# A macaron decoder layer in split fp32: the spatial output is computed earlier and parked in DRAM, and eight pairs of the mixer's merge run on seven products at three units a block

## The chip, the cores and the metric

The kernel runs on one core of a Trainium2 chip. The metric is the device time of one execution in microseconds. The version before takes 1982.98 us, the median of three runs (1982.88 to 1983.88). One more execution was profiled.

## The reference

One layer of a hybrid decoder on 256 tokens of width 2048, in float32:

```
x = x + 1/2 * SwiGLU_1(rms(x))              # D_FF = 5632
h = rms(x); h @ w_in -> q | k | v | u | v_sg | gate_att | gate_sg
    A: causal dilated window attention, 3 groups of 4 heads (dilations 1, 4, 16),
       partial rotary, the groups of a head slot merged by their softmax denominators
    B: u * (W_s LN(v_sg) + b), W_s lower-triangular, 12 groups      @ w_sg_out -> y_sg
x = x + (sigmoid(gate_att) * (A @ w_att_out) + sigmoid(gate_sg) * y_sg) @ w_out
x = x + 1/2 * SwiGLU_2(rms(x)); final RMSNorm
```

Nearly all of the work is in the matrix products. x stays in SBUF for the whole layer; the weights are read from DRAM once, in order.

## The kernel before, in words

**A product.** TensorE (PE) multiplies in a reduced fp32 format. To keep fp32 accuracy each weight tile w is split on the chip into wh, a rounded copy made by ScalarE (ACT, L356), and wl = w - wh, made by VectorE (DVE, a subtraction recorded at the helper line L66). The activations are split into xhi and xlo in the same way. A product is then three matmuls, wh x xhi, wl x xhi and wh x xlo, each with 512 output columns in one PSUM bank (`product`, L363). A *unit* is one weight tile of 128x512.

**Gemms and steps.** `gemm` notes each matrix product as a row of column blocks of 512; `lay_out` then writes the whole program as one list of steps. A plain step ("n") covers two units and both token halves: 12 matmuls. One such step is one *tick*; callbacks are hung at ticks with `at(tick, fn)`. The engines run their instructions in the order in which this loop issues them, and so does SP, which issues nearly all the DMAs.

**Quads.** Two gemms on the same activations and a run of k tiles form a 2x2 block product: two token halves, two column blocks, two k halves. `quad_products` runs it in the Strassen-Winograd way on seven products p1 to p7 in place of eight. `nq` says how many pairs of k tiles the blocks hold; the rest of the pair's k tiles run as plain steps in between. A product is one "s" step of nq units and 3 x nq matmuls. The blocks of weights lie in a *home* (room in SBUF); DVE makes four further forms of them (`prepare`: f, t2, t1, t4, recorded as `sum<-quads`, `quads<-sum,quads` and the like), and forms of the activations are made by `sums_of` when x is turned. ACT and DVE also move three of the partial results between PSUM banks and a small tile (`read` in `quad_products`); p5 may only begin when DVE has read p7's bank. Opening products (p1, p6, p7) are put some steps ahead of the pair's own first step, closing ones (p5, p4, p3, p2) into it.

**The ring.** wh and wl live in a ring of nine units (`RING`). `advance` splits steps a few ahead of PE as long as the ring's room is free, that is, as PE has gone past the units that lay there. Raw weights come in by SP two units at a time (512 KB, L256), five such tiles ahead (`RAWB`); quad blocks come in by `load_block` (L298).

**Turns.** x, and other matrices that PE needs transposed, go through DRAM: DVE transposes blocks of 32 (`btx<-x`), SP writes them out (`bmx<-btx`) and reads them back with the blocks exchanged (`xt<-bmx`), ACT scales them, and ACT and DVE split them into xhi and xlo.

**The mixer.** Column blocks of w_in in the order vs, u (with a home of their own, `gates`), q and k of three groups, v, then for each chunk c of 512 columns gs, w_sg_out, ga, w_att_out; then w_out. `merge` is the second home: gs/ga for c = 2, 3 and the two pairs of w_out run there as quads with nq = 2. Attention (`attention`, L938 ff.) starts 16 ticks behind the last k and takes a head slot every five ticks: scores into two banks (`qk`, recorded as sc, L951), `softmax` (DVE and ACT), the turn of p through DRAM, ten ticks later the product with v (`pv`, L986 ff.) into one bank, and a tick behind that the split of the result into oT (`oev`). All these banks come in turn from `tp_bank`, four of the eight PSUM banks.

Of the kernel before, what the change touches and what calls it, by code (L numbers as in the profile page):

```python
# [18 lines left out]
P = 128  # L19
# [20 lines left out]
CS = (2, 0, 0)  # L40
CM = 2
# [30 lines left out]
def layer(ctx: ExitStack, tc: tile.TileContext, a, out):  # L72
# [10 lines left out]

    def tp_bank(name):
        return ps.tile([P, NC], F32, tag="tp", bufs=4, name=name)
# [11 lines left out]

    rows = sb.tile([64, P], F32, name="rows")
# [15 lines left out]
    x = big.tile([P, NT, D], F32, name="x")  # L114
    xv = a["x"][0].rearrange("(t p) d -> p t d", p=P)

    def load_x(c0, c1):
        SP.dma_start(x[:, :, c0:c1], xv[:, :, c0:c1])
# [26 lines left out]
    def opening(count):  # L145
        return zip((5, 3, 1) if count > 9 else (4, 2, 1), ("p1", "p6", "p7"))

    def lay_out():
        i, count = 0, 0
        while i < len(gemms):  # L150
# [23 lines left out]
            count = len(order) if size > 1 else 16  # L174
# [87 lines left out]
    def ffn_home(home):  # L262
        home["h"] = [big.tile([P, 16, S], F32R, tag=tag, name=f"h{tag}") for tag in "AB"]
# [12 lines left out]
    def merge_home(home):  # L276
        l_ = sb.tile([P, 3, 2, NC], F32, tag="L", name="quads")
        w = sb.tile([P, 3, NC], F32, tag="W", name="part")
        t = sb.tile([P, 2, NC], F32, tag="tmp", bufs=2, name="sum")
        return l_[:, 0], l_[:, 1], l_[:, 2], w[:, 1:3], t, l_[:, 0], w[:, 0]  # L280

    def move_in(home):
        home["room"] = home["make"](home)
        for b in (0, 2, 3, 1):
            load_block(next(q for q in quads if q["home"] is home), b)
# [107 lines left out]
    def quad_products(i, quad, form):  # L393
# [5 lines left out]
        for q in range(quad["nq"]):  # L399
# [6 lines left out]
            else:  # L406
                hi, lo = (v[:, ("p5", "p6", "p7", "p3").index(form)] for v in quad["forms"]["forms"][q])
# [111 lines left out]
    def norm_squares(n, c):  # L519
        for t in range(NT):  # L520
            ACT.activation(junk, x[:, t, c * NC:(c + 1) * NC], AF.Square, accum_out=ss[n][:, t, c:c + 1])
# [18 lines left out]
    def first_transposes(k):  # L540
        b = first_place(k)
        for t in range(NT):
            PE.transpose(b[:, t * P:(t + 1) * P], x[:, t, k * P:(k + 1) * P], ident)
# [5 lines left out]

    def residual(e, n, c, banks, scale, norm):  # L550
        cs = slice(c * NC, (c + 1) * NC)

        def add():
            for t in range(NT):
                DVE.scalar_tensor_tensor(two(x[:, t, cs]), banks[t], scale, two(x[:, t, cs]),
# [11 lines left out]

        turn_x(e + (6 if c == 1 else 2), n, c, (9 if n == 1 else 7) if c == 3 else 6)

    def turn_x(i, n, c, lag, read=3):  # L570
        def evac(src):
# [6 lines left out]
            if c == CS[n]:  # L578
                sums_of(i + lag, xT, 0, 2, forms_tile(big, "oT", f"fx{n}", 2), src, f"x{n}", tag)
            elif n != 1 and c == CS[n] + 1:  # L580
                sums_of(i + lag, xT, 2, 1, forms_tile(big, "k2", f"fy{n}", 1), src, f"y{n}", tag)

        turn(i, f"x{n}_{c}", 8, put_tokens(lambda: x[:, :, c * NC:(c + 1) * NC]),
# [8 lines left out]
    def ffn(wg, wu, wd, down_post, group):  # L592
# [7 lines left out]
        def lhs_h():  # L600
            return home["h"]

        for after, (part, quads_of) in zip(GATES, enumerate(PARTS)):
            for f in range(*after):
# [13 lines left out]
                def post_up(e, banks, st=st, f=f, kl=kl, quads_here=quads_here):  # L618
# [11 lines left out]
                    def ev(src):  # L630
                        hi, lo = (v[:, kl:kl + 4] for v in home["h"])
# [19 lines left out]
                quad = dict(k0=4 * CS[n], nq=2 if late else 3, forms=xT, home=merge if late else home)  # L651
                gemm(wg, f * NC, 0, KD, lhs_x, post_gate, BOTH if f else LATE, bank, quad)
                gemm(wu, f * NC, 0, KD, lhs_x, post_up, BOTH, bank, quad)
            for c in range(4):
                if c % 2 == 0:
                    bank = side()
                    quad = dict(k0=quads_of["k0"], nq=quads_of["nq"], forms=sets[part], home=home)
# [143 lines left out]
    def spatial(e):  # L801
        for pg in range(6):
            got = {}

            def prod(pg=pg, got=got):
                if pg == 0:
                    both = [big.tile([P, 16, S], F32R, tag=tag, name=f"uT{tag}") for tag in "BA"]
                    mix["uT"] = [v[:, 0:NG] for v in both]
                    mix["fs"] = [v[:, NG:].rearrange("p f (q t) -> p f q t", q=2) for v in both]
# [29 lines left out]
    def post_qk(key, gi):  # L839
        def post(e, banks):  # L840
# [4 lines left out]
            if (key, gi) == ("q", 0):  # L845
                parts = big.tile([P, 4, one], F32R, tag="E", name="qk0")
                kept = xT["both"]

                def keep():
                    for new, old in zip(mix["fs"], kept):  # L850
                        ACT.activation(new, old.bitcast(F32), AF.Copy)
                    mix["forms"] = {q: [v[:, :, q] for v in mix["fs"]] for q in range(2)}
# [3 lines left out]
            elif (key, gi) == ("q", 1):  # L856
# [3 lines left out]
                mix["q", 2] = sb.tile([P, one], F32, tag="W", name="q2")  # L860
# [77 lines left out]
    def attention(e):  # L938
        for s in range(NSLOT):
            got = {}  # L940
            e0 = e + 5 * s
# [3 lines left out]
            def qk(s=s, got=got):  # L945
                got["b"] = [tp_bank(f"sc{s}_{r}") for r in range(2)]
# [31 lines left out]
            def pv(s=s, got=got):  # L978
                bank = got["o"] = tp_bank(f"pv{s}")
# [18 lines left out]
            for k, f in ((0, qk), (1, softmax), (10, pv), (11, oev)):  # L998
# [3 lines left out]
    def post_sig(key):  # L1002
# [20 lines left out]
    def post_merge(c):  # L1023
        def post(e, banks):
# [11 lines left out]
            def ev(src):  # L1036
                split_psum(turned(mix["mhi"][:, 4 * c:4 * c + 4]), turned(mix["mlo"][:, 4 * c:4 * c + 4]), src, c < 2)
                if c == CM:
                    sums_of(e + 10, mix, 0, 2, lambda: mix["fs"], src, "m", "tmp")
# [6 lines left out]
    for j, (c0, post) in enumerate(front):  # L1046
# [3 lines left out]
        if j % 2 == 0:  # L1050
            bank = side()
            quad = dict(k0=4 * CS[1], nq=2, forms=xT, home=gates)
# [4 lines left out]
    for gi in (1, 2, 0):  # L1057
        gemm(w_in, o_v + gi * NC, 0, KD, lhs_x, post_v(gi))
    sg_out = lambda: mix["uT"]
    att_out = lambda: (mix["oT"][:, 0], mix["oT"][:, 1])  # L1060
    for c in range(4):
        if c < 2:
            bank = (mm_bank, tp_bank)[c]
            gemm(w_in, o_gs + c * NC, 0, KD, lhs_x, post_sig("gs"), bank=bank)
            gemm(a["w_sg_out"][0], c * NC, 0, NG, sg_out, post_mul("gs"), bank=bank)
            gemm(w_in, o_ga + c * NC, 0, KD, lhs_x, post_sig("ga"), bank=bank)
        else:
            sides[0] += c == 2
            bank = side()
            quad = dict(k0=4 * CS[1], nq=2, forms=mix, home=merge)  # L1070
            gemm(w_in, o_gs + c * NC, 0, KD, lhs_x, post_sig("gs"), BOTH, bank, quad)
            gemm(w_in, o_ga + c * NC, 0, KD, lhs_x, post_sig("ga"), BOTH, bank, quad)
            gemm(a["w_sg_out"][0], c * NC, 0, NG, sg_out, post_mul("gs"), bank=bank)
        gemm(a["w_att_out"][0], c * NC, 0, NSLOT, att_out, post_merge(c), bank=bank)
    for c in range(4):
        if c % 2 == 0:
            bank = side()
            quad = dict(k0=4 * CM, nq=2, forms=mix, home=merge)
        gemm(a["w_out"][0], c * NC, 0, KD, lambda: (mix["mhi"], mix["mlo"]),
             lambda e, banks, c=c: residual(e, 2, c, banks, 1.0, True), PAIR if c == 0 else BOTH, bank, quad)  # L1080

# [4 lines left out]
    def down2(e, c, banks, last):  # L1086
# [5 lines left out]
        def add():  # L1092
            if c == 0:
                ss[3] = sb.tile([P, NT, 5], F32, name="ss3")
            for t in range(NT):
                DVE.scalar_tensor_tensor(two(x[:, t, cs]), banks[t], 0.5, two(x[:, t, cs]),
                                         op0=OP.mult, op1=OP.add)
            norm_squares(3, c)
            for t in range(NT):
                DVE.tensor_tensor(x[:, t, cs], x[:, t, cs], fin["g"][:, cs], op=OP.mult)  # L1100
# [9 lines left out]
    def finish(t):  # L1110
# [3 lines left out]
        for q, cs in enumerate((a_, b_)):  # L1114
            DVE.scalar_tensor_tensor(x[:, t, cs], bank[:, q], 0.5, x[:, t, cs], op0=OP.mult, op1=OP.add)
# [196 lines left out]
```

## Time and profile before

| | |
|---|---|
| median of 3 runs | 1982.98 us |
| profiled execution | 1985.29 us |
| span in the profile | 1983.5 us |
| mean granted TensorE clock | 0.999 of full |
| PE / PE weight loads / DVE / ACT / POOL busy | 99 / 87 / 80 / 60 / 3% |
| DRAM traffic | 461 MB read, 30 MB written, 247 GB/s |

The profiled execution takes 1.8 us more than its span. In a view of groups each row gives line, engine, operation, output and inputs by the program's names, how often it occurs, its busy time and the mean ns of one, and then the idle time ahead of these instructions with what ended it. In a timeline each row gives start and length in us; a bracket is the idle time before the row and what released it. Rows of the trace are of the profiled execution.

### The profile page before, as it was taken

To read this page: it belongs to the slowest core of one execution; us is meant where nothing else is said; L and a number is where in the kernel's file an instruction comes from. 1 tells how busy PE (TensorE), PEld (TensorE's weight loads), DVE (VectorE), ACT (ScalarE), POOL (GpSimd) and SP (SyncE) were. 2 spreads that over 40 slices of the span, in tenths; PEclk is the share of its full clock that TensorE was granted. 3 is DMA by queue.
4 is the path that set the end of the run, shared out by engine and by line. 5 is a ranking of instruction groups with operands and counts; after the bars stand their busy time and mean duration, and the time that the engine had idled before them with its cause. 6 is when DMAs were issued, how large, how long until landed. Compare 5 with 4: busy or idle time off the path is not lost.

```text
span 1983.5 us, 25183 instructions
## 1 busy us (share of the span) xinstructions
PE 1971.1 (99%) x9188; PEld 1723.6 (87%) x9188; DVE 1592.2 (80%) x1655; ACT 1189.5 (60%) x1382; POOL 51.7 (3%) x48
## 2 busy tenths in 40 slices
PE   9999999999999999999999999999999999999998
PEld 8888888888888888888888888878888888888887
DVE  6798888888897798766665777888898889888886
ACT  7566556665666676555454555576655566565664
POOL 0000100000000000000000000000000000000000
PEclk9999999999999999999999999999999999999999
DMA  9788778787777985888877667788888777878783
GB/s 323 256 279 271 237 238 266 247 254 245 247 242 226 289 294 186 254 275 255 264 238 249 210 204 231 237 260 267 255 252 260 234 249 247 252 250 254 244 265 123
DMA packets 264644, 492.34 MB, mean 248 GB/s; under 512 B 17484, under 2 KB 46024, under 8 KB 264392
## 3 DMA queue, kind: packets, MB, share of 16 engines
q1 hardware_dynamic: 253624, 469.49, 72.0%
q0 software_dynamic: 10576, 20.71, 6.0%
q8 instruction: 72, 1.18, 0.2%
q10 hardware_dynamic: 320, 0.53, 0.1%
q14 instruction: 52, 0.43, 0.1%
HBM read 461.01 MB, written 29.66 MB: 247 GB/s over the span
## 4 chain that ended last, share of the span: by engine, by line
PE 95%; DVE 2%; DMA 1%; issue 1%; ACT 0%; SPq 0%; POOLq 0%; POOL 0%; DVEq 0%; ACTq 0%
PE qd L363 71%; PE mm L363 22%; DVE wl L66 1%; DMA raw<-in_w_in_dram 0%; DMA quads<-in_w_in_dram 0%; DVE btx L66 0%; ACT wh L356 0%; PE sp L815 0%; PE warm L1180 0%; DMA xt<-bmx 0%; DVE xlo L66 0%; PE pv L990 0%; PE sc L953 0%; DVE x L66 0%; DVE quads L66 0%
## 5 line engine op out<-in xcount | busy, mean ns | idle before, releaser
L66 DVE TENSOR_TENSOR wl<-raw,wh 128x1024 fp32r<-128x1024 f32 (+1 forms) x636 | 695.7, 1112 | 184.5 <-ACT wh L356 182.8
L356 ACT ACTIVATE wh<-raw 128x1024 fp32r<-128x1024 f32 (+1 forms) x636 | 609.1, 966 | 365.8 <-PE qd L363 199.6
L363 PE MATMUL qd<-wh,xlo 128*128 128x512 f32 x1201 | 455.4, 379 | 1.0 <-DVE xlo L66 1.0
L363 PE MATMUL qd<-wh,xhi 128*128 128x512 f32 x1201 | 455.3, 379 | 0.0
L363 PE MATMUL qd<-wl,xhi 128*128 128x512 f32 x1201 | 455.2, 379 | 0.0
L356 ACT ACTIVATE wh<-quads 128x1536 fp32r<-128x1536 f32 (+2 forms) x226 | 250.9, 1117 | 271.1 <-PE qd L363 251.5
L66 DVE TENSOR_TENSOR wl<-quads,wh 128x1536 fp32r<-128x1536 f32 (+2 forms) x226 | 291.0, 1301 | 147.7 <-ACT wh L356 147.5
L363 PEld LDWEIGHTS qd<-wh,xlo 128*128 128x128 f32 x1201 | 227.0, 189 | 33.9 <-DVE xlo L66 1.8
L363 PEld LDWEIGHTS qd<-wh,xhi 128*128 128x128 f32 x1201 | 227.0, 189 | 32.4 <-issue 0.2
L363 PEld LDWEIGHTS qd<-wl,xhi 128*128 128x128 f32 x1201 | 227.0, 189 | 32.2
L363 PE MATMUL mm<-wh,xlo 128*128 128x512 f32 x608 | 230.6, 379 | 0.9 <-DVE xlo L66 0.8
L363 PE MATMUL mm<-wh,xhi 128*128 128x512 f32 x608 | 231.1, 380 | 0.1
L363 PE MATMUL mm<-wl,xhi 128*128 128x512 f32 x608 | 228.5, 379 | 0.0
L363 PE MATMUL qd<-wh,hA 128*128 128x512 f32 x564 | 213.8, 379 | 0.0
L363 PE MATMUL qd<-wl,hA 128*128 128x512 f32 x564 | 213.8, 379 | 0.0
L363 PE MATMUL qd<-wh,hB 128*128 128x512 f32 x564 | 213.8, 379 | 0.0
L356 ACT ACTIVATE wh<-sum 128x1024 fp32r<-128x1024 f32 (+2 forms) x85 | 101.4, 1196 | 86.7 <-PE qd L363 66.9
L66 DVE TENSOR_TENSOR wl<-sum,wh 128x1024 fp32r<-128x1024 f32 (+2 forms) x85 | 117.8, 1395 | 18.0 <-ACT wh L356 16.5
L363 PEld LDWEIGHTS mm<-wh,xlo 128*128 128x128 f32 x608 | 114.9, 189 | 17.8 <-DVE xlo L66 1.6
L363 PEld LDWEIGHTS mm<-wh,xhi 128*128 128x128 f32 x608 | 114.9, 189 | 16.2 <-ACT xhi L547 0.2
L363 PEld LDWEIGHTS mm<-wl,xhi 128*128 128x128 f32 x608 | 114.9, 189 | 16.1
L363 PE MATMUL qd<-wh,fx 128*128 128x512 f32 x352 | 119.2, 379 | 1.0 <-DVE part L66 1.0
(417 smaller groups left out, 2191.2 us busy)
## 6 DMA issues: line engine op xcount, KB each, us to landing
raw<-in_w_in_dram SPq DMA_DIRECT2D x168, 512.0 KB, 4.9
raw<-in_ffn_w_down_dram SPq DMA_DIRECT2D x120, 512.0 KB, 5.0
raw<-in_ffn_w_up_dram SPq DMA_DIRECT2D x112, 512.0 KB, 6.0
raw<-in_ffn_w_gate_dram SPq DMA_DIRECT2D x111, 512.0 KB, 4.2
quads<-in_ffn_w_gate_dram SPq DMA_DIRECT2D x38, 768.0 KB, 6.4
quads<-in_ffn_w_up_dram SPq DMA_DIRECT2D x38, 768.0 KB, 5.1
quads<-in_ffn_w_down_dram SPq DMA_DIRECT2D x32, 512.0 KB, 5.4
quads<-in_ffn_w_up_dram POOLq DMA_DIRECT2D x17, 768.0 KB, 10.6
```

The lines of the kernel that those rows point to most:

```text
L66: return method(out, *args, **kwargs)
L356: ACT.activation(wh, r[:, first:end], AF.Copy)
L363: PE.matmul(g["ps"][t], act, in_turn(w), start=not g["begun"][t], stop=g["left"][t] == 0, skip_group_check=g["quad"] is not None)
```

## The change

**Order.** The four w_sg_out gemms run ahead of the second q. Their results y go to DRAM (`post_sg`, four tiles yd of 512 KB) and come back one chunk at a time (`load_y`), to be multiplied with sigmoid(gs).

**Room.** x is written to DRAM chunk by chunk at the end of FFN1 (`out_x`), its SBUF room holds forms of x during the mixer (`forms_room`, filled in part by copies in `keep`), and x is read back behind the last gs (`load_old_x`, four times 512 KB). The home `merge` moves from three small tiles to the two large ones A and B, which w_sg_out has left; q2 and y lie in the rest of B.

**Quads.** merge now has eight pairs, all with nq = 3: q2/k2, v1/v2, the four gs/ga and the two of w_out. With it go 48 of 9022 matmuls of 512 columns; 48 units more are split on ACT and DVE. In `prepare` and the splits, 70 more DVE instructions have 1536 columns and 47 fewer have 1024. The x forms for the mixer's quads are made from chunks 2 and 3 in place of 0 and 1 (`CS`), those for w_out from 1 and 2 in place of 2 (`CM`).

**Attention.** It starts 13 ticks behind the last k, takes a head every four ticks, and `tp_bank` is split: scores and pv share the two banks of `lo_bank`, the other two are `hi_bank`. Behind pv of heads 2 and 3 stands one matmul of constants into the unused half of the bank.

```diff
-CS = (2, 0, 0)
-CM = 2
+CS = (2, 2, 0)
+CM = 1
...
+    halves = [0]
+
     def tp_bank(name):
-        return ps.tile([P, NC], F32, tag="tp", bufs=4, name=name)
+        halves[0] += 1
+        return (lo_bank, hi_bank)[(halves[0] - 1) // 2 % 2](name)
+
+    def lo_bank(name):
+        return ps.tile([P, NC], F32, tag="tp", bufs=2, name=name)
+
+    def hi_bank(name):
+        return ps.tile([P, NC], F32, tag="tq", bufs=2, name=name)
...
     def opening(count):
+        if count == 4:
+            return zip((2, 1, 0), ("p1", "p6", "p7"))
...
     def merge_home(home):
-        l_ = sb.tile([P, 3, 2, NC], F32, tag="L", name="quads")
-        w = sb.tile([P, 3, NC], F32, tag="W", name="part")
-        t = sb.tile([P, 2, NC], F32, tag="tmp", bufs=2, name="sum")
-        return l_[:, 0], l_[:, 1], l_[:, 2], w[:, 1:3], t, l_[:, 0], w[:, 0]
+        a_, b_ = (big.tile([P, 4096], F32, tag=tag, name=f"quads{tag}") for tag in "AB")
+        t = sb.tile([P, SGW], F32, tag="W", name="sum")
...
+        home["left"] = b_[:, 2 * SGW:]
+        return b11, b21, b12, b22, t2, b11, a_[:, 2 * SGW:2 * SGW + NC]
...
+        if n == 1:
+            def out_x():
+                old_x[c] = m = dram.tile([P, NT, NC], F32, tag=f"xd{c}", name=f"xd{c}")
+                SP.dma_start(m, now_x[0][:, :, cs])
+
+            at(e + 5, out_x)
...
-                attention(e + 16)
-                at(e + 16 + 15 + 12, lambda: move_in(merge))
+                attention(e + 13)
+                at(e + 29, lambda: load_y(0))
...
-            e0 = e + 5 * s
+            e0 = e + 4 * s
...
-                got["b"] = [tp_bank(f"sc{s}_{r}") for r in range(2)]
+                got["b"] = [lo_bank(f"sc{s}_{r}") for r in range(2)]
...
-                bank = got["o"] = tp_bank(f"pv{s}")
+                bank = got["o"] = lo_bank(f"pv{s}")
...
+                if s > 1:
+                    PE.matmul(bank[:, S:NC], ones[:, 0:P], ones[:, 0:S], start=False, stop=True, skip_group_check=True)
...
-            for k, f in ((0, qk), (1, softmax), (10, pv), (11, oev)):
+            o = max(10, 12 - 4 * s)
+            for k, f in ((0, qk), (1, softmax), (o, pv), (o + 1, oev)):
...
+            at(e + 1, go)
+            at(e + 2, lambda: SP.dma_start(m, y))
+            if c == 3:
+                at(e + 1, lambda: move_in(merge))
...
+            if key == "gs":
+                at(e + 2, lambda: DVE.tensor_tensor(t_, t_, mix["y"], op=OP.mult))
+                if c < 3:
+                    at(e + 4, lambda: load_y(c + 1))
+                else:
+                    at(e + 1, lambda: load_old_x(e + 1))
...
-    for gi in range(3):
+    for gi in range(2):
+        if gi == 1:
+            for c in range(4):
+                gemm(a["w_sg_out"][0], c * NC, 0, NG, sg_out, post_sg(c), bank=(lo_bank, hi_bank, mm_bank, mm_bank)[c])
...
+    quad = x_quad()
+    gemm(w_in, o_q + 2 * NC, 0, KD, lhs_x, post_qk("q", 2), BOTH, tp_bank, quad)
+    gemm(w_in, o_k + 2 * NC, 0, KD, lhs_x, post_qk("k", 2), BOTH, tp_bank, quad)
...
+    for gi in (1, 2):
+        gemm(w_in, o_v + gi * NC, 0, KD, lhs_x, post_v(gi), BOTH, mm_bank, quad)
+    gemm(w_in, o_v, 0, KD, lhs_x, post_v(0), bank=hi_bank)
     for c in range(4):
...
+        quad = x_quad()
+        gemm(w_in, o_gs + c * NC, 0, KD, lhs_x, post_sig("gs", c), BOTH, bank, quad)
+        gemm(w_in, o_ga + c * NC, 0, KD, lhs_x, post_sig("ga", c), BOTH, bank, quad)
...
-            quad = dict(k0=4 * CM, nq=2, forms=mix, home=merge)
+            bank = (mm_bank, tp_bank)[c // 2]
+            quad = dict(k0=4 * CM, nq=3, forms=lambda: mix, home=merge)
```

**What moves.** PE where the scores of head 3 are formed (pv is a head's product with v, sc_0 and sc_1 are the two banks of its scores, mm is a plain gemm, qd a quad's bank). Before, between two plain steps, with pv of head 1 ahead of them:

```order
L363 MATMUL mm_1_7307<-wh,xlo_4564 128x512
L986 MATMUL pv_7465<-pTk,vq 128x256
L987 MATMUL pv_7465<-pTk,vq 128x2x64
L990 MATMUL pv_7465<-pTk,vq 128x128 x4
L951 MATMUL sc_0_7472<-qk_6004 128x256 x3
L953 MATMUL sc_0_7472<-pTk,vq 128x128
L953 MATMUL sc_0_7472<-k_6346,q_6345 128x128
L951 MATMUL sc_1_7473<-qk_6004 128x256 x3
```

Now, with pv of head 0 ahead of them and p5 of the first gs/ga quad ahead of that:

```order
L377 MATMUL qd_3_7624<-wh,fy_5175 128x512
L1025 MATMUL pv_7841<-pTk,vq 128x256
L1026 MATMUL pv_7841<-pTk,vq 128x2x64
L1029 MATMUL pv_7841<-pTk,vq 128x128 x4
L990 MATMUL sc_0_7848<-qk_6020 128x256 x3
L992 MATMUL sc_0_7848<-pTk,vq 128x128
L992 MATMUL sc_0_7848<-k_6787,quadsB 128x128
L990 MATMUL sc_1_7849<-qk_6020 128x256 x3
```

The bank of sc_1 is now that of pv_7841, a few rows ahead of it; sc_0 has the other of the two.

DVE where the result of pv of head 0 is read (oT<-pv; p is a head's scores in SBUF, btp their transposed blocks). Before, from the end of head 1's softmax:

```order
L66 TENSOR_SCALAR p_7255<-p_7255,ar_7262 128x512 x2
L66 TENSOR_TENSOR wl<-raw_7168,wh 128x1024
L66 TENSOR_TENSOR wl<-raw_7188,wh 128x1024
L66 STREAM_TRANSPOSE btp_7298<-p_7255 128x8x4x32
L66 TENSOR_TENSOR wl<-raw_7206,wh 128x1024
L66 COPY pTk<-p_7137 128x512
L66 TENSOR_TENSOR wl<-raw_7235,wh 128x1024
L66 TENSOR_TENSOR wl<-raw_7266,wh 128x1024
L66 TENSOR_TENSOR oT<-pv_7340,oT 128x2x128
```

Now, from the end of head 2's softmax:

```order
L66 TENSOR_SCALAR p_7772<-p_7772,ar_7779 128x512 x2
L66 TENSOR_TENSOR wl<-quadsA,wh 128x512
L66 TENSOR_TENSOR wl<-quadsA,wh 128x1024
L66 TENSOR_TENSOR wl<-raw_7634,wh 128x1024
L66 TENSOR_TENSOR quadsA<-quadsA,qd_3_7624 128x512
L66 STREAM_TRANSPOSE btp_7822<-p_7772 128x8x4x32
L66 TENSOR_TENSOR wl<-sum,wh 128x1536
L66 TENSOR_TENSOR wl<-raw_7665,wh 128x1024
L66 TENSOR_TENSOR wl<-raw_7709,wh 128x1024
L66 TENSOR_TENSOR qd_2_7623<-qd_3_7624,quadsA 128x512
L66 TENSOR_TENSOR oT<-pv_7841,oT 128x2x128
```

The same read comes one head later, and steps of a quad (quadsA, sum, qd) stand among the splits.

SP at the start of the mixer, around the last quarter of x (xt_3) and the load of the first quad's blocks. Before:

```order
L256 DMA raw_4969<-in_w_in_dram 128x2x512
L482 DMA xt_3_4989<-bmx_3_4927 32x4x256 x4
L256 DMA raw_4994<-in_w_in_dram 128x2x512
L298 DMA quads<-in_w_in_dram 128x2x512 x4
L256 DMA raw_5017<-in_w_in_dram 128x2x512
```

Now:

```order
L268 DMA raw_4975<-in_w_in_dram 128x2x512
L592 DMA xd_4995<-x 256x1x512
L496 DMA xt_3_4997<-bmx_3_4925 32x4x256 x4
L268 DMA raw_5002<-in_w_in_dram 128x2x512
L312 DMA quads<-in_w_in_dram 128x2x512 x4
L268 DMA raw_5025<-in_w_in_dram 128x2x512
```

The write of x's last quarter (xd) stands ahead of both; that of the third quarter stands ahead of xt_2 in the same way.

More of the change, by code (lines that the diff above doesn't have):

```diff
@@ L846, in post @@
                 parts = big.tile([P, 4, one], F32R, tag="E", name="qk0")
-                kept = xT["both"]
+                kept, room = xT["fx"], xT["forms_room"]
                 def keep():
-                    for new, old in zip(mix["fs"], kept):
-                        ACT.activation(new, old.bitcast(F32), AF.Copy)
-                    mix["forms"] = {q: [v[:, :, q] for v in mix["fs"]] for q in range(2)}
+                    for k in range(2):
+                        ACT.activation(room[:, k, :, 0:2], kept[k].bitcast(F32), AF.Copy)
+                    xT["kept"] = dict(forms={q: [room[:, k, :, q] for k in range(2)] for q in range(3)})
                 at(e + 4, keep)
@@ L1051, in layer, with x_quad @@
             bank = side()
-            quad = dict(k0=4 * CS[1], nq=2, forms=xT, home=gates)
+            quad = dict(k0=4 * CS[1], nq=2, forms=lambda: xT, home=gates)
         gemm(w_in, c0, 0, KD, lhs_x, post, BOTH, bank, quad)
-    for gi in range(3):
+    sg_out = lambda: mix["uT"]
+    att_out = lambda: (mix["oT"][:, 0], mix["oT"][:, 1])
+    def x_quad():
+        return dict(k0=4 * CS[1], nq=3, forms=lambda: xT["kept"], home=merge)
+    for gi in range(2):
+        if gi == 1:
+            for c in range(4):
+                gemm(a["w_sg_out"][0], c * NC, 0, NG, sg_out, post_sg(c), bank=(lo_bank, hi_bank, mm_bank, mm_bank)[c])
@@ L1173, in layer @@
     wb = tp_bank("warm")
-    ones = nc.const_aps.tensor(1.0, [P, NC], BF16)
     def keep_warm(count, w=NC):
```

117 lines of the change are left out of this document (68 added, 49 removed).

## The prediction

> **What bounds the kernel now.** The profile's page was read first: the span, the busy shares of the engines, and the chain that ended last.
>
> ```profile
> span 1983.5 us, 25183 instructions
> PE 1971.1 (99%) x9188; PEld 1723.6 (87%) x9188; DVE 1592.2 (80%) x1655; ACT 1189.5 (60%) x1382; POOL 51.7 (3%) x48
> PE 95%; DVE 2%; DMA 1%; issue 1%; ACT 0%; SPq 0%; POOLq 0%; POOL 0%; DVEq 0%; ACTq 0%
> ```
>
> A busy PE is not yet a PE at its limit, so the next view is the chain of waits in order of time, for the distance between matmuls in a long unbroken piece, and then what PE waited for in the whole run (us in total, times, longest).
>
> ```profile
> 96.55 543.91 PE qd L363 x2520
> ```
> ```profile
> PE qd L363 <- DVE part L66: 1.0, 1, 1.0
> PE qd L363 <- DVE xlo L66: 1.0, 2, 0.8
> ...
> PE mm L363 <- DVE xlo L66: 0.8, 1, 0.8
> PE qd L363 <- DVE wl L66: 0.6, 1, 0.6
> ```
>
> 543.91 us for 2520 matmuls is 0.2158 us each, without a break. The waits on DVE sum to 3.4 us. So PE sets the time: a matmul taken out is worth 0.2158 us, as long as no engine that feeds PE comes late. Whether one does is read by stage. Columns: busy time of PE, PEld, DVE, ACT and POOL, granted clock, DMA share, GB/s.
>
> ```profile
> 660.00:680.00 20.00, 20.00 (x95) 17.50 (x93) 12.23 (x13) 14.55 (x24) 0.00 (x0) 1.00 0.91 279
> 680.00:700.00 20.00, 19.16 (x89) 16.48 (x88) 14.45 (x17) 11.05 (x16) 1.10 (x1) 1.00 1.02 351
> 960.00:980.00 20.00, 20.00 (x101) 17.72 (x100) 14.48 (x20) 11.13 (x18) 0.00 (x0) 1.00 0.78 243
> 1000.00:1020.00 20.00, 20.00 (x108) 17.91 (x107) 13.22 (x16) 11.28 (x16) 0.00 (x0) 1.00 0.74 206
> 1040.00:1100.00 60.00, 60.00 (x280) 52.54 (x279) 37.70 (x38) 28.63 (x32) 0.00 (x0) 1.00 0.72 234
> 1240.00:1290.00 50.00, 50.00 (x233) 43.80 (x232) 42.67 (x47) 30.19 (x38) 0.00 (x0) 1.00 0.76 236
> 1310.00:1330.00 20.00, 18.37 (x83) 15.48 (x84) 19.96 (x27) 17.72 (x29) 0.00 (x0) 1.00 0.79 237
> ```
>
> The clock is full throughout. Attention (960 to 1020) and the gates behind it leave DVE a quarter to a third idle; the end of w_out (1240) leaves 15%; the step into FFN2 (1310) leaves nothing, and there PE already loses 1.6 us. The start of the mixer (680) is bound by DMA: a share of 1.02, and PE loses 0.8 us.
>
> **The change, part by part.** *Matmuls.* A pair on seven products saves 3 x nq matmuls. Four pairs at nq 2 become eight at nq 3: 72 saved in place of 24, so 48 fewer, 48 x 0.2158 = 10.4 us, less 0.2 for the two small constant matmuls: **-10.1 us**. The row above prices a matmul. The Trainium skill, TensorE: Matmul & The Clock Gate, Back-to-back issue gap, gives a sustained 131 ns for a matmul of 512 columns in a stream with weight loads, and 216 only for one by itself. By 131 ns the 48 would be worth an estimated 6.3 us; this trace runs 2520 of them in such a stream at 216, so the measured price stands.
>
> *DVE and ACT.* A pair that becomes a quad of nq 3 costs 9 more units of 512 columns on both engines and four prepares on DVE. The groups by line, with shapes kept apart (busy us, mean ns):
>
> ```profile
> L66 DVE TENSOR_TENSOR wl<-raw,wh 128x1024 fp32r<-128x1024 f32 x506 | 613.5, 1222 | 179.7 <-ACT wh L356 177.9
> L66 DVE TENSOR_TENSOR wl<-quads,wh 128x1536 fp32r<-128x1536 f32 x88 | 154.6, 1757 | 105.0 <-ACT wh L356 105.0
> ...
> L66 DVE TENSOR_TENSOR wl<-raw,wh 128x512 fp32r<-128x512 f32 x130 | 84.5, 685 | 4.9 <-ACT wh L356 4.9
> ...
> L66 DVE TENSOR_TENSOR sum<-quads 128x1536 f32<-128x1536 f32 x23 | 40.3, 1752 | 0.0
> ...
> L66 DVE TENSOR_TENSOR oT<-pv,oT 128x256 fp32r<-128x256 f32 x4 | 1.9, 469 | 3.9 <-ACT oT L461 3.9
> ```
> ```profile
> L356 ACT ACTIVATE wh<-quads 128x1536 fp32r<-128x1536 f32 x88 | 130.5, 1483 | 179.1 <-PE qd L363 177.5 <-PE mm L363 1.7
> ```
>
> Now attention, for one head on DVE and on PE (start, length):
>
> ```profile
> 958.89 1.35 DVE L66 SCALAR_TENSOR_TENSOR p<-sc,mask 128x512 f32<-128x512 f32 x2
> 960.28 1.22 DVE L66 TENSOR_REDUCE am<-p 128x2 f32<-128x1024 f32 x1
> 963.08 0.17 DVE L66 RECIPROCAL ar<-am 128x2 f32<-128x2 f32 x1 [1.59 <-ACT p L964]
> 963.28 0.88 DVE L66 TENSOR_SCALAR p<-p,ar 128x512 f32<-128x512 f32 x2
> 965.17 2.36 DVE L66 TENSOR_TENSOR wl<-raw,wh 128x1024 fp32r<-128x1024 f32 x2 [1.01 <-ACT wh L356]
> 967.45 1.24 DVE L66 STREAM_TRANSPOSE btp<-p 128x1024 f32<-128x1024 f32 x1
> ```
> ```profile
> 957.75 0.52 PE L951 MATMUL sc<-qk 128*128 128x256 f32 x3
> ...
> 958.47 0.60 PE L951 MATMUL sc<-qk 128*128 128x256 f32 x3
> ...
> 959.27 0.46 PE L363 MATMUL mm<-wh,xhi 128*128 128x512 f32 x1
> ```
> ```profile
> 986.86 0.59 PE L986 MATMUL pv<-pTk,vq 128*128 128x256 f32 x2
> ...
> 988.33 0.60 PE L951 MATMUL sc<-qk 128*128 128x256 f32 x3
> ```
>
> Two 1024-column splits take 2.36 us, not 2.44: in a row, each starts 0.08 us before the last one's end. So a step of DVE is 1.14 us at 1024 columns, 1.67 at 1536, 0.60 at 512, 1.16 for the transpose; a softmax holds DVE from 958.89 to 964.16, 5.2 us with its wait for ACT. On PE a head's scores take 1.52 us (half of them 0.72) and pv 1.47.
>
> *Attention is the large term.* In the new order the second half of head 3's scores goes into the bank that pv of head 0 has just filled, so PE must wait until DVE has read it (the oT row). DVE gets there in its own order. The work before it begins with the split of p1 of the first gs/ga quad, whose room in the ring of nine comes free when PE reaches head 0's scores. From there to the oT row, by the new order: seven instructions of 1536 columns (4 splits, 3 prepares) 11.7 us, eight of 1024 9.1, seven of 512 4.2, three softmaxes 15.6, three transposes 3.5, a copy and the oT step 0.8: 44.9, and 1.5 for ACT's copy ahead of the first. PE meanwhile has 144 matmuls 31.1, three heads' scores 4.6, pv 1.5 and half of head 3's scores 0.7: 37.9. PE waits 46.4 - 37.9 = **8.5 us**; its p5 step just ahead of that waits for the same queue, so this is counted once. Before, heads came every five ticks, the steps between were plain ones, and four banks took turns. Low end: without the three waits of 1.59 for ACT, 3.7. High end: a wait for ACT's weight copy of 1.0 behind each softmax, as at 965.17, 11.5. The sum is nearest to the middle. The Trainium skill, Perfetto Trace Analysis, Matmuls, asks for groups to rotate through PSUM banks so that one's evacuation lies beside the next one's matmuls, which speaks against four banks becoming two. The rule by itself would price only the exposed evacuation, some 0.5 us of DVE by the oT row; here the queue ahead of the evacuation is the cost.
>
> *Start of the mixer.* Four transfers of 512 KB write x to DRAM; the last two stand on SP ahead of the last x turns and of the four quad loads, in the stretch where DMA is full.
>
> ```profile
> 671.69 1.71 ACT L574 ACTIVATE xt<-xt,gcols 128x256 f32<-128x256 f32 x4 [3.67 <-DMA raw<-in_w_in_dram]
> ...
> 689.22 1.06 ACT L356 ACTIVATE wh<-quads 128x1024 fp32r<-128x1024 f32 x1 [6.24 <-DMA quads<-in_w_in_dram]
> ```
>
> At 351 GB/s one is 1.5 us, two 3.0. ACT already waits here for both. The sums for the x forms, now from chunks 2 and 3, fall into this stretch too, but DVE idles 5.5 of 20 us there. From 0 to 5 us; I take half of the two transfers, **+1.5**.
>
> *Gates and w_out.* A gs/ga pair with its att_out is 207 matmuls, 44.7 us. At the share of the row at 1040 (0.63) DVE works 28.1 us of that; 9 units (half of 1.14 each, 5.1) and four prepares (4 x 1.67, 6.7) make it 39.9, a share of 0.89, little above the 0.85 that the row at 1240 bears without a stall. y's reading back and its product with the gate (one 1024-column step a chunk) lie in the same gaps; the transfers have a DMA share of 0.72 to hide in. **+0.5**, from 0 to 3. Moving the spatial output ahead, ACT's 16 copies more and the second reading of x are covered likewise (ACT 60% busy, PE never waiting for it between 720 and 1300).
>
> *Step into FFN2.*
>
> ```profile
> 1298.54 1.23 DVE L66 TENSOR_TENSOR wl<-raw,wh 128x1024 fp32r<-128x1024 f32 x1 [4.16 <-ACT wh L356]
> ...
> 1326.75 0.68 DVE L66 TENSOR_TENSOR part<-part,qd 128x512 f32<-128x512 f32 x1
> ```
>
> From 1298.54 on DVE has no idle time up to the last wait of PE. The second w_out quad at nq 3 adds four times 0.53 for the prepares, three units (1.7), and takes 0.6 from PE's time: up to 4.4 us. A part of it lies before 1298, where DVE is idle for 4.16 us: **+1.5**, from 0 to 4.4.
>
> Sum: -10.1 + 8.5 + 1.5 + 0.5 + 1.5 = +1.9 us.
>
> **The rivals.** *The full gain.* Attention's wait does not form, because DVE, a third idle there now, has worked ahead. Against it: the ring holds nine units, so DVE cannot be ahead by more than those, and the sum starts at that limit. Then -10.1 with the 3.5 of the other terms: 1976.4, and 1972.9 without them. It decides if all waits together stay under 6.
>
> *Slower by the DMA at the start of the mixer.* The two writes of x push the x turns and the quad loads back by their whole length and the sums of the x forms follow on DVE: 5 us in place of 1.5, so +5.4 and 1988.4 by the median. For it: the share of 1.02 and PE's loss of 0.8 there now. Against it: 9% of the engines' time is free in the 20 us before. It decides if PE's loss between FFN1 and the second gemm of the mixer grows by over 3.6 us.
>
> *Slower by attention.* ACT's copies queue behind its exponentials: 11.5 in place of 8.5, so +4.9, 1987.9. For it: the waits of 1.0 above.
>
> That the products are not dropped is excluded by the instruction order.
>
> **How the numbers follow.** The profiled execution took 1985.3 us (span 1983.5 and 1.8 around it), 2.3 above the median of 1982.98. Forecast: 1985.3 + 1.9 - 2.3 = 1984.9. About 0.2% (4 us) is what a measurement of this kernel can tell from no change; so "same" is 1979 to 1987, which is a sum of the waits from 6 to 14 us. Forecast 0.47; full gain 0.27, since the largest term rests on rows in an order that no trace shows yet; slower by DMA 0.13, by attention 0.13. All terms at their low ends give -6.4 (1976.6), all at their high ends +14.3. The full gain's case runs from 1972.9 to 1979, so the range goes down to 1974.5, which leaves out about a third of it (0.09); up to 1992 it takes in both slower cases but for their far ends (0.06).
>
> **What would show it.** Right: PE waits of some 8 us in attention, at p5 of the first gs/ga quad and at the second half of head 3's scores, put down to DVE; PE's busy time near 1961; a wait of 1 to 2 us more at 680 to 700 and at 1300 to 1330. Wrong: no PE gap over 2 us in attention (then the gain stands), or gaps of 4 us or more at the mixer's start with ACT waiting for quads.

## The result and the profile after

The changed kernel takes 2010.24 us (median of 4 runs, 2008.43 to 2012.1) against 1983.43 us before (4 runs): a ratio of 1.0135, interval 1.0117 to 1.0152, 27 us slower. The forecast was 1984.9 in a range that ended at 1992, so it was wrong, and on the side on which I had put a quarter of the chance (0.26, of which 0.06 lay beyond the range). The profiled execution took 2012.1 us.

The page of the changed kernel, its span, the busy shares and the engines of the chain that ended last:

```profile
span 2010.4 us, 25130 instructions
PE 1971.9 (98%) x9142; PEld 1717.9 (85%) x9142; DVE 1656.0 (82%) x1691; ACT 1217.1 (61%) x1410; POOL 53.6 (3%) x48
PE 86%; DVE 6%; DMA 3%; issue 2%; ACT 2%; SPq 0%; DVEq 0%; POOLq 0%; POOL 0%; ACTq 0%
```

PE has fewer matmuls and the same busy time, where the forecast had looked for 1961. The next views say why: what PE waited for, then the stretches in which it did (the same columns as before the change), and two of these stretches in the kernel before.

```profile
PE qd L377 <- DVE xlo L66: 7.5, 2, 6.4
PE qd L377 <- ACT qd L433: 5.7, 1, 5.7
PE qd L377 <- DVE wl L66: 2.9, 4, 1.3
PE qd L377 <- ACT wh L370: 2.6, 1, 2.6
PE qd L377 <- DVE mlo L66: 2.0, 1, 2.0
PE qd L377 <- ACT quadsA L431: 1.7, 1, 1.7
PE pv L1025 <- DVE pTk L66: 1.6, 1, 1.6
...
PE sc L990 <- DVE oT L66: 1.0, 1, 1.0
```
```profile
600.00:720.00 120.00, 117.04 (x537) 100.65 (x536) 90.58 (x102) 78.43 (x108) 1.63 (x1) 1.00 0.85 272
960.00:1000.00 40.00, 38.36 (x177) 32.97 (x176) 36.29 (x47) 24.54 (x28) 0.00 (x0) 1.00 0.80 253
1000.00:1115.00 115.00, 105.00 (x519) 91.70 (x518) 88.74 (x93) 64.65 (x86) 0.00 (x0) 0.97 0.72 235
1200.00:1250.00 50.00, 47.47 (x210) 40.35 (x209) 45.16 (x45) 31.25 (x36) 0.00 (x0) 0.97 0.78 267
1300.00:1365.00 65.00, 53.20 (x227) 44.48 (x226) 50.30 (x62) 40.50 (x59) 0.51 (x1) 0.92 0.70 215
```
```profile
1000.00:1115.00 115.00, 115.00 (x556) 101.33 (x555) 71.46 (x74) 58.13 (x70) 0.00 (x0) 1.00 0.73 231
1300.00:1365.00 65.00, 62.44 (x285) 53.14 (x284) 61.45 (x69) 46.37 (x66) 1.05 (x1) 1.00 0.79 259
```

Two things are to be seen. PE is idle in five places, not one. And in three of them the granted clock (behind POOL's column) is below 1.00, which it was in none of the stretches before: PE is busy there, but slowly. PE's start-to-start distances in the trace show both. A matmul of 512 columns takes 0.216; what a distance has above that is lost. Summed by place, from the traces of the two kernels (us; a distance counts from 0.235 up):

| place | before | after | more | forecast |
|---|---|---|---|---|
| start of the mixer, 600 to 720 | 1.1 | 4.5 | 3.4 | 1.5 |
| q2/k2, 960 to 1000 | 0.2 | 2.2 | 2.0 | none |
| attention, 1000 to 1115 | 0.2 | 13.6 | 13.4 | 8.5 |
| gates and w_out, 1115 to 1300 | 0.0 | 6.0 | 6.0 | 0.5 |
| step into FFN2, 1300 to 1365 | 3.8 | 16.4 | 12.6 | 1.5 |
| all | 5.4 | 42.7 | 37.4 | 12.0 |

37.4 lost against 10.1 gained is 27.3; the spans differ by 26.9. The gain is there, then, and the losses are three times the forecast.

**Attention.** Timelines of the changed kernel, first ACT, then PE, then DVE (start, length; in brackets the idle time before and its releaser):

```profile
1056.78 0.72 ACT L1003 ACTIVATE p<-p,am 128x512 f32<-128x512 f32 x1 [5.40 <-DVE am L66]
...
1058.21 1.56 ACT L370 ACTIVATE wh<-quadsA 128x512 fp32r<-128x512 f32 x2
1059.68 1.04 ACT L370 ACTIVATE wh<-raw 128x1024 fp32r<-128x1024 f32 x1
1060.62 0.57 ACT L433 ACTIVATE qd<-qd 128x512 f32<-128x512 f32 x1
```
```profile
1061.25 0.79 PE L377 MATMUL qd<-wh,xhi 128*128 128x512 f32 x1 [5.68 <-ACT qd L433]
1061.84 0.63 PE L377 MATMUL qd<-wl,xhi 128*128 128x512 f32 x1
1062.26 0.63 PE L377 MATMUL qd<-wh,xlo 128*128 128x512 f32 x1
1062.69 0.63 PE L377 MATMUL qd<-wh,xhi 128*128 128x512 f32 x1
...
1065.25 0.44 PE L377 MATMUL qd<-wh,fy 128*128 128x512 f32 x1
```
```profile
1062.20 0.68 DVE L66 TENSOR_TENSOR quadsA<-quadsA,qd 128x512 f32<-128x512 f32 x1
...
1070.29 0.41 DVE L66 TENSOR_TENSOR oT<-pv,oT 128x256 fp32r<-128x256 f32 x1
```

The longest wait ends with ACT's copy of p7's result (L433). The matmul that waits belongs to a plain step of the pair, which adds to the bank that this copy fills; p5 (the row with fy) comes behind it. ACT was not busy: it waited 5.4 us for DVE's row maximum of head 2, and the copy stood behind the exponentials of that head in ACT's order. DVE was where the forecast's sum put it, late by the splits, prepares and softmaxes ahead; but the first to feel it was ACT, on behalf of PE. The wait at oT, which the sum had priced, is only 1.0, since PE had already lost the time. And the matmuls behind the wait start 0.43 us apart, not 0.216.

**Step into FFN2.** DVE, ACT and PE in turn:

```profile
1299.69 1.29 DVE L66 STREAM_TRANSPOSE btx<-x_again 128x512 f32<-128x512 f32 x2
...
1308.43 1.23 DVE L66 TENSOR_TENSOR wl<-raw,wh 128x1024 fp32r<-128x1024 f32 x1
1319.62 1.76 DVE L66 TENSOR_TENSOR wl<-quadsB,wh 128x1536 fp32r<-128x1536 f32 x1 [9.97 <-ACT wh L370]
...
1330.83 1.22 DVE L66 TENSOR_TENSOR xlo<-xt,xhi 128x1024 fp32r<-128x1024 f32 x1
```
```profile
1315.42 1.70 ACT L601 ACTIVATE xt<-xt,gcols 128x256 f32<-128x256 f32 x4 [7.03 <-DMA xt<-bmx]
...
1318.12 1.47 ACT L370 ACTIVATE wh<-quadsB 128x1536 fp32r<-128x1536 f32 x1
```
```profile
1319.64 0.48 PE L377 MATMUL qd<-wh,mhi 128*128 128x512 f32 x1 [2.62 <-ACT wh L370]
...
1332.10 0.80 PE L377 MATMUL qd<-wh,xlo 128*128 128x512 f32 x1 [6.40 <-DVE xlo L66]
1332.68 0.63 PE L377 MATMUL qd<-wh,xhi 128*128 128x512 f32 x1
```

DVE, full since 1277, transposes x's first quarter at 1299.7. Its turn through DRAM lands at 1315.4. ACT stands still for 7 us meanwhile, in order, and with it the copies of the weights; DVE stands still for 10 us behind ACT. The first copy that stands behind the turn (1318.12) is of the w_out quad's own last product, p2, and PE waits 2.6 us for it. When DVE goes on, prepares and forms lie ahead of xlo, and PE waits 6.4 us for that. In the kernel before, the same turn reads, on DVE and then on ACT:

```profile
1280.96 1.30 DVE L66 STREAM_TRANSPOSE btx<-x 128x512 f32<-128x512 f32 x2
```
```profile
1290.44 1.06 ACT L356 ACTIVATE wh<-quads 128x1024 fp32r<-128x1024 f32 x1 [0.51 <-PE qd L363]
...
1294.76 1.71 ACT L574 ACTIVATE xt<-xt,gcols 128x256 f32<-128x256 f32 x4 [1.10 <-DMA xt<-bmx]
...
1297.46 1.04 ACT L356 ACTIVATE wh<-raw 128x1024 fp32r<-128x1024 f32 x1
```

There the last split of the w_out quad (1290.44) stands ahead of the turn in ACT's order, not behind it. From the first transpose to ACT's scaling the turn took 13.8 us; now it took 15.7.

### The profile page after: what moved, and what is told of

Read it like the earlier page. It is cut to its first block, busy times and chain, and to the rows that moved or that the text cites. A ratio compares the mean times of both kernels' runs of the same rounds, so it can differ in the third digit from the quotient of the medians.

```text
span 2010.4 us, 25130 instructions
## 1 busy us (share of the span) xinstructions
PE 1971.9 (98%) x9142; PEld 1717.9 (85%) x9142; DVE 1656.0 (82%) x1691; ACT 1217.1 (61%) x1410; POOL 53.6 (3%) x48
## 4 chain that ended last, share of the span: by engine, by line
PE 86%; DVE 6%; DMA 3%; issue 2%; ACT 2%; SPq 0%; DVEq 0%; POOLq 0%; POOL 0%; ACTq 0%
PE qd L377 73%; PE mm L377 13%; DVE wl L66 3%; ACT wh L370 1%; DVE sum L66 1%; DMA raw<-in_w_in_dram 0%; DMA quadsB<-in_ffn_w_up_dram 0%; DMA xt<-bmx 0%; DVE quadsA L66 0%; DMA quadsB<-in_w_out_dram 0%; DMA raw<-in_w_att_out_dram 0%; DMA bmx<-btx 0%; DMA raw<-in_ffn_w_down_dram 0%; ACT xt L601 0%; DVE btx L66 0%
## 5 line engine op out<-in xcount | busy, mean ns | idle before, releaser
L377 PE MATMUL qd<-wh,xhi 128*128 128x512 f32 x1387 | 528.1, 381 | 6.0 <-ACT qd L433 5.7
L377 PE MATMUL qd<-wl,xhi 128*128 128x512 f32 x1387 | 527.6, 380 | 0.0
L370 ACT ACTIVATE wh<-sum 128x1536 fp32r<-128x1536 f32 (+2 forms) x98 | 117.3, 1203 | 105.2 <-PE qd L377 75.2
L66 DVE TENSOR_TENSOR wl<-sum,wh 128x1536 fp32r<-128x1536 f32 (+2 forms) x98 | 136.2, 1401 | 16.4 <-ACT wh L370 15.4
L377 PE MATMUL mm<-wh,xlo 128*128 128x512 f32 x352 | 133.6, 380 | 1.5 <-DVE xlo L66 1.5
L377 PE MATMUL mm<-wh,xhi 128*128 128x512 f32 x352 | 133.9, 381 | 0.2 <-ACT xhi L561 0.2
L377 PE MATMUL mm<-wl,xhi 128*128 128x512 f32 x352 | 131.9, 380 | 1.5 <-DVE wl L66 1.5
L377 PEld LDWEIGHTS qd<-wh,hB 128*128 128x128 f32 x564 | 106.6, 189 | 15.1
L377 PEld LDWEIGHTS qd<-wh,hA 128*128 128x128 f32 x564 | 106.6, 189 | 15.1
L377 PEld LDWEIGHTS qd<-wl,hA 128*128 128x128 f32 x564 | 106.6, 189 | 15.1
```

Source lines behind the costliest of these rows:

```text
L66: return method(out, *args, **kwargs)
L370: ACT.activation(wh, r[:, first:end], AF.Copy)
L377: PE.matmul(g["ps"][t], act, in_turn(w), start=not g["begun"][t], stop=g["left"][t] == 0, skip_group_check=g["quad"] is not None)
```

## The experiments

The theory after these traces: PE's losses are DVE's own work queued in order, a quad's splits and prepares ahead of what frees a bank, a ring place or a turn of x. The rivals are the two shared PSUM banks, the added transfers, and DVE's order (not the amount of its work). Each edit below is of the changed kernel unless said otherwise. "Lost" is counted as in the table, for the execution with a profile. The ratios are to runs of the kernel before that were taken with each experiment; their medians lie between 1983.98 and 1984.96 us.

**The low part of x at once** (`turn_x`, ahead of FFN2 only):

```diff
-            split_psum(hi, lo, src, 1 if n and c < 3 else 0)
+            split_psum(hi, lo, src, 1 if n == 1 and c < 3 else 0)
```

> The changed kernel with one edit: in the turns of x ahead of FFN2 the low part xlo is made as soon as the high part is there, not up to a tick later. The changed kernel takes 2010.2 us; PE loses 16.4 us between 1300 and 1365 us there, 6.9 of it in one wait for xlo. Theory order (the low part stands behind prepares and forms in DVE's queue, and PE waits for it): the wait of 6.9 and its half-clock matmuls go, and PE loses 7 to 10 us in that stretch, total 2002 to 2005. Rival load (DVE has too much to do there, whatever the order): the wait for xlo turns into a wait for a split of the same length within 2 us, total 2008 to 2011. Rival transfer (the x turn's DMA lands late): the first wait of 3.0 at 1319 stays and is followed by others, loss 13 or more.

Measured: 2005.02 us, ratio to before 1.0104 (1.0089 to 1.0119). The wait of 6.4 for xlo went, and no matmul there ran at the half rate any more, but others took its place; lost from 1300 to 1365: 11.5, where I had expected 7 to 10. Five executions with the order unchanged there (the changed kernel, and the edits to gs/ga, q2/k2, the writes and the reading back) lost 13.1 to 16.4, so the order explains 2 to 5 of the 12.6, not all.

**A shorter second w_out quad:**

```diff
-            quad = dict(k0=4 * CM, nq=3, forms=lambda: mix, home=merge)
+            quad = dict(k0=4 * CM, nq=2 if c else 3, forms=lambda: mix, home=merge)
```

> The changed kernel with nq 2 in place of 3 in the second pair of w_out: three matmuls more (0.6 us), three units and 2.1 us of prepares less on DVE ahead of FFN2. Theory load (the longer quad makes DVE late at the step into FFN2): the loss between 1300 and 1365 falls from 16.4 to 6 to 9 us, total 2002 to 2005. Theory order: it falls by no more than the 4 us of DVE work, to 12 to 15, total 2007 to 2010.

Measured: 1999.03 us, ratio 1.0074 (1.0057 to 1.0091). Lost in that stretch: 2.5, less than before the change. The length of the second quad is the cause; I had expected a part of the loss to stay. Timelines of this kernel, DVE and ACT, and its window:

```profile
1292.69 1.30 DVE L66 STREAM_TRANSPOSE btx<-x_again 128x512 f32<-128x512 f32 x2
...
1309.05 1.23 DVE L66 TENSOR_TENSOR wl<-raw,wh 128x1024 fp32r<-128x1024 f32 x1 [2.94 <-ACT wh L370]
```
```profile
1302.16 1.06 ACT L370 ACTIVATE wh<-quadsB 128x1024 fp32r<-128x1024 f32 x1 [0.51 <-PE qd L377]
...
1305.29 1.69 ACT L601 ACTIVATE xt<-xt,gcols 128x256 f32<-128x256 f32 x4
```
```profile
1300.00:1365.00 65.00, 63.34 (x291) 54.34 (x290) 58.30 (x67) 46.78 (x68) 1.06 (x1) 1.00 0.85 273
```

The transpose comes 7.0 us earlier, some 2.5 of which this execution had gained further ahead. ACT finds its data there (no bracket), and DVE's 10 us of standing still become 2.9. So a quad that made DVE some 4.5 us late had cost 14. Not all of that is shown to be the lateness: with the shorter quad ACT's copy for p2 (1302.16) also stands ahead of the x turn again, as in the kernel before, and the turn takes at most 12.6 us in place of 15.7. No run separates these.

**The first gs/ga pair as plain steps:**

```diff
-        quad = x_quad()
+        quad = x_quad() if c else None
         gemm(w_in, o_gs + c * NC, 0, KD, lhs_x, post_sig("gs", c), BOTH, bank, quad)
```

> The changed kernel with the first gs/ga pair as plain steps: nine matmuls more (1.9 us), and on DVE nine units and four prepares less beside attention. PE loses 13.6 us between 1000 and 1115 now. Theory queue (the quad's work stands ahead of the softmaxes and of the reads that free banks on DVE): the loss falls under 4 us, total 2000 to 2003. Rival banks (two banks for scores and pv in place of four make PE wait whatever stands beside them): the loss stays over 7, total 2006 to 2012.

Measured: 1998.69 us, ratio 1.0073 (1.0058 to 1.0088). Its window:

```profile
1000.00:1115.00 115.00, 114.83 (x578) 101.46 (x577) 85.54 (x95) 66.23 (x86) 0.00 (x0) 1.00 0.79 256
```

Lost there: 1.1, with the two shared banks and a head every four ticks still in place. The quad beside attention was the cause. (The total is below the 2000 to 2003 expected; this execution also lost 2.4 less at the start of the mixer and 3.3 less at the step into FFN2.)

**The shared banks alone, in the kernel before:** `tp_bank`, `lo_bank` and `hi_bank` as in the change, and

```diff
-                got["b"] = [tp_bank(f"sc{s}_{r}") for r in range(2)]
+                got["b"] = [lo_bank(f"sc{s}_{r}") for r in range(2)]
...
-                bank = got["o"] = tp_bank(f"pv{s}")
+                bank = got["o"] = lo_bank(f"pv{s}")
```

> The kernel before with one part of the change: scores and pv of attention share two PSUM banks, the other two are kept for the rest; heads still every five ticks, plain steps beside them. PE loses 0.2 us between 950 and 1045 in the kernel before. Theory queue (the shared banks cost only what stands ahead of the reads on DVE): the second half of a head's scores waits for the pv just ahead of it, some 1 to 2 us at two or three places, 2 to 5 in all, total 1985 to 1989. Rival banks: 8 us or more, total over 1991. A loss under 1 would say that the banks are free.

Measured: 1984.92 us, ratio 1.0001 (0.9991 to 1.0010), PE idle 0.15 us in each of the two stretches:

```profile
960.00:1000.00 40.00, 39.85 (x203) 35.31 (x202) 29.24 (x37) 21.99 (x35) 0.00 (x0) 1.00 0.78 241
1000.00:1115.00 115.00, 114.85 (x554) 101.10 (x553) 70.96 (x73) 57.75 (x70) 0.00 (x0) 1.00 0.75 229
```

The rival falls, and my own figure of 2 to 5 us with it: beside plain steps two banks cost nothing that can be measured. No run has the quad beside attention with four banks; in the changed kernel the wait at the shared bank itself is 1.0 us.

**No writes of x** (the residual of the mixer is read back from the input, so the first FFN is left out of it):

```diff
-                old_x[c] = m = dram.tile([P, NT, NC], F32, tag=f"xd{c}", name=f"xd{c}")
-                SP.dma_start(m, now_x[0][:, :, cs])
+                old_x[c] = xv[:, :, cs]
```

> The changed kernel without the four writes of x to DRAM; the residual of the mixer is read back from the layer's input, so that the reads stay (this leaves out the first FFN in the residual). PE loses 4.5 us between 600 and 720 now, 1.1 before the change. Theory transfer (the writes push the x turns and the quads' loads back): 1 to 2 us there, total 2006 to 2008. Rival forms (the sums for the x forms, now from the last two quarters of x, are late on DVE): 3.5 to 4.5 as now, total 2009 to 2012.

Measured: 2005.88 us, ratio 1.0112 (1.0097 to 1.0127). Lost from 600 to 720: 0.4, less than before the change (1.1):

```profile
600.00:720.00 120.00, 120.00 (x556) 104.55 (x555) 94.22 (x108) 80.48 (x110) 1.63 (x1) 1.00 0.84 267
```

So the writes cause this loss, not the forms, as far as one execution can show it. Its size is loose: six profiled executions with the same order there (the changed kernel, and the edits to xlo, w_out, gs/ga, q2/k2 and the reading back) lost 1.6 to 4.5 us.

**x read back later:**

```diff
-                    at(e + 1, lambda: load_old_x(e + 1))
+                    at(e + 8, lambda: load_old_x(e + 8))
```

> The changed kernel with one edit: the reading back of x begins seven ticks later, behind the last att_out's weights. PE loses 5.0 us between 1200 and 1250 in the changed kernel, 3.9 of it in a wait at 1239 and its half-clock matmuls, where the att_out weights took 7.6 us to land beside the first read of x. Theory transfer: the loss there falls to 1 to 2, and nothing grows elsewhere, total 2005 to 2007. Rival prepares (DVE comes late at that place because of the w_out quad's prepares, which follow the wait): the loss stays over 4, total 2009 to 2011.

Measured: 2010.96 us, ratio 1.0136 (1.0121 to 1.0151). Lost from 1200 to 1250: 5.0 as in the changed kernel, and 2.2 more than there between 1250 and 1300. The reading of x was not the cause. The chain of waits had named the att_out weights' DMA, and these took 7.7 us to land here too; but DVE works without a gap from 1229.8 to mlo, with the quad's splits and prepares ahead of it, so its queue is what is left.

**q2/k2 as plain steps:**

```diff
-    quad = x_quad()
+    quad = None
     gemm(w_in, o_q + 2 * NC, 0, KD, lhs_x, post_qk("q", 2), BOTH, tp_bank, quad)
```

> The changed kernel with q2/k2 as plain steps: nine matmuls more, 1.9 us. PE loses 2.2 us between 960 and 1000 in the changed kernel and nothing before the change. If this quad's work on DVE is the cause, the loss goes and the two cancel: total 2009 to 2011. If the cause lies elsewhere (rotary and turns of q and k, moved closer together), the loss stays and the total is 2011 to 2013.

Measured: 2010.5 us, ratio 1.0124 (1.0107 to 1.0140). Lost from 960 to 1000: 0.0. As a quad this pair wins 1.9 us and loses 2.2.

**Several edits together.** First the plain gs/ga pair, the shorter second w_out quad, x read back later, and

```diff
-            at(e + 5, out_x)
+            at(e + (5 if c < 2 else 8), out_x)
```

> Four edits together: the first gs/ga pair plain, the second w_out pair at nq 2, x read back seven ticks later, the writes of its last two quarters three ticks later. If the losses are separate, the lost time falls from 42.7 by 12.5 (attention), 13.9 (step into FFN2), 3.5 (x read back) and 3 (mixer start) to some 10 us, and 12 matmuls come back (2.6 us): a span of 1978 to 1982, total 1980 to 1984, level with the kernel before. If they are one chain whose slack moves on, the lost time stays over 18 us and the total over 1988.

Measured: 1986.7 us, ratio 1.0010 (1.0000 to 1.0019), 11.9 us lost in all: the losses are separate. The total is above the 1980 to 1984 that I had expected, and the profiled execution's span, 1982.9, just above its 1978 to 1982. With nq 2 for q2/k2 besides (`quad = x_quad(2)`, with nq as an argument of `x_quad`):

> As the kernel with four edits, and q2/k2 at nq 2 in place of 3: three matmuls more (0.6 us) and less on DVE there. If the loss of 2.2 us at q2/k2 comes from the quad's load on DVE it falls under 0.7, and this runs 0.5 to 1.5 us faster than the kernel with four edits; otherwise 0.6 slower.

Measured: 1985.57 us, ratio 1.0004 (0.9995 to 1.0013), lost from 960 to 1000: 0.0, in all 11.0. Whether it is faster than the version with four edits the runs cannot tell. With nq 2 for both w_out pairs besides (`nq=2, forms=lambda: mix, home=merge`):

> The kernel with five edits (the four, and q2/k2 at nq 2), and both w_out pairs at nq 2. Three matmuls more (0.6 us). PE still loses 2.1 us at the low part of the merged activations, behind the first w_out quad's prepares, and 0.9 ahead of it. If that load is the cause, both fall under 1 together: span 1980 to 1981, a gain of 1 to 2 us. If the turn of the merged activations sets it, the loss stays and the span is 1982 to 1983.

Measured: 1982.83 us, ratio to before 0.9991 (0.9982 to 1.0000), lost 8.5. Its window at the merged activations:

```profile
1200.00:1250.00 50.00, 50.00 (x234) 43.80 (x233) 46.18 (x50) 30.61 (x36) 0.00 (x0) 1.00 0.74 247
```

The wait there is gone, so it was the first w_out quad at nq 3, with its longer prepares and splits ahead of the low part. This version has 30 matmuls fewer than the kernel before and is at best a little faster than it, at the edge of what the runs can tell. The low part of every x turn at once, in this version and in the kernel before (`split_psum(hi, lo, src, 0)`):

> As the kernel before it in this list, and the low part of every x turn made at once. PE loses 2.2 us at the mixer's start in a wait for xlo and 3.4 at the step into FFN2. If DVE's order is the cause, both fall by 1 to 2 us and the span is 1977 to 1979; if the load is, the wait moves to a split of the weights and the span stays within 0.5 us.

> The kernel before with the low part of every x turn made at once. PE loses 1.1 us at the mixer's start and 3.8 at the step into FFN2 there, most of it in waits for xlo. If the order is the cause, 1 to 3 us less, a total of 1980 to 1982; if the load is, within 0.5 us of the kernel before.

Measured: 1984.52 us, 0.9998 (0.9989 to 1.0006), and 1986.04 us, 1.0004 (0.9995 to 1.0013). Neither gains. In the kernel before, the lost time at the step into FFN2 went from 3.8 to 3.1 and that at the mixer's start from 1.1 to 3.6; in the other version the start went from 2.0 to 3.9. The delay of the low part seems to serve the start, by one execution of each.

## Why the prediction was wrong

- *The price of a matmul and the 48 fewer* held: the lost time and -10.1 together give the difference of the spans to within 0.4 us.
- *Attention, 8.5 (3.7 to 11.5), measured 13.4.* The mechanism was right, as the plain gs/ga pair shows, and the term too small. The sum ran to one reader of DVE's queue, the oT row; PE waited earlier, for copies of ACT's whose turn hung on the same queue (1.7 at 1050, 5.7 at 1061), and later again for p's turn (1.6 at pv). The half rate behind the long wait added 1.7. The bank that I had put at the centre accounts for 1.0 of it.
- *Step into FFN2, 1.5 (0 to 4.4), measured 12.6.* This is the step that failed. I let most of DVE's extra work vanish in the 4.16 us in which DVE stood idle before 1298. That idle time was no reserve: DVE was waiting for ACT, and ACT for x's turn, which starts with a transpose in DVE's own queue. Work ahead of the transpose delays the end of the idle time by at least as much: from the transpose to that end it is 17.6 us before, 19.9 in the changed kernel and 16.4 with the shorter quad. The shorter quad took the loss from 16.4 to 2.5; the order on DVE (xlo behind prepares) is 2 to 5 us of it. How the rest divides between DVE's lateness, ACT's copy for p2 behind the turn and a slower turn stays open.
- *Gates and w_out, 0.5 (0 to 3), measured 6.0, and 2.0 at q2/k2, not priced at all.* A share of 0.89 over 45 us says nothing of the moment at which four prepares come together ahead of one small step that PE needs: mlo at 1239 (2.0, and seven matmuls at the half rate). The first w_out quad at nq 2 removes that wait.
- *Start of the mixer, 1.5 (0 to 5), measured 3.4* in one execution, 0.5 to 3.4 in six: the cause was right, and the size within its bounds.
- *The rivals.* The slower cases had 0.26, each as one place that goes worse. What happened was the forecast's own mechanism, work queued in order ahead of what PE needs, at four places at once, and the writes of x at the fifth. The high ends of the terms add up, with the -10.1, to +13.8, not to the +14.3 of the prediction, and three of them were themselves too low: the terms measured 13.4, 12.6 and 6.0 against high ends of 11.5, 4.4 and 3.
- *The half rate behind long waits*, 5.5 us in all, had no term.

## What to carry to other kernels

An engine's idle time is cover only if it does not end with something that begins in that engine's own queue; follow what ends it back to its start before putting work into it. Where two engines feed a third in order, look for the first instruction of either that waits on the late queue, not for the last one in it. And a busy share is to be read over the length of the slack (here a ring of nine units; at six matmuls a unit in plain steps and three in a quad's, an estimated 6 to 12 us of PE), not over the whole stage. A longer block can also change an order: with three units a product, the last split of the w_out quad fell behind the x turn in ACT's queue.

## What the runs showed of the hardware

After a wait PE may run on at half its rate. Behind the waits of 5.7 and 6.4 us, and of 2.0 at 1239, the matmuls started 0.427 us apart in place of 0.216 for 5 to 8 matmuls, as they did behind two waits of 2.6 and 1.3 close together, and the clock granted from 1320 to 1340 was 0.74:

```profile
1239.02 0.48 PE L377 MATMUL qd<-wh,mlo 128*128 128x512 f32 x1 [1.97 <-DVE mlo L66]
...
1240.07 0.63 PE L377 MATMUL qd<-wh,xlo 128*128 128x512 f32 x1
1240.50 0.63 PE L377 MATMUL qd<-wh,xhi 128*128 128x512 f32 x1
```
```profile
1320.00:1340.00 20.00, 12.29 (x41) 9.75 (x41) 18.37 (x23) 8.69 (x11) 0.00 (x0) 0.74 0.51 158
```

In the changed kernel 26 matmuls ran so, 5.5 us of the 42.7; behind the waits of 1.6 to 1.7 us none did, and in the first version with several edits none did behind one of 2.0 either, so the length of the wait alone does not decide. In the version with q2/k2 as plain steps up to 13 matmuls in a row ran so, 5.6 us. The Trainium skill, TensorE: Matmul & The Clock Gate, The HAM clock gate, says that PE's clock is halved after an idle window of about 3.4 us, which runs free of the program, and comes back after at least one busy window. The half rate agrees with these rows; the wait of 2.0 at 1239, shorter than a window, is more than that rule gives, and five matmuls at the half rate (2.1 us) are less than a window. So a wait of several us cost 1.1 to 1.7 us more than itself in the changed kernel (5 to 8 matmuls, 0.211 each), which the forecast had left out.
